# Sixteen query weights fetched and split by two GpSimd transfers each, in a two-block transformer kernel on one core

## The chip, the cores and the metric

The kernel runs on one core of a Trainium2 chip. The core has TensorE (matmuls), VectorE, ScalarE, GpSimd and SyncE, each with an instruction queue of its own that is worked off in order, and 16 DMA engines that all queues share. The metric is the device time of one execution in microseconds (us), lower is better.

## The reference

Two transformer blocks follow each other on 256 tokens of width 1024, all in float32. The part that the change touches is the first block's pair of attentions: a windowed one with grouped queries and a differential one. Cut to that part:

```python
def first_block(x, meta_tokens, pre_mix_gain, w_in, ...):
    h = concatenate([filler, meta, x], axis=1)
    u = rms_norm(h, pre_mix_gain)
    qa, ka, va, qb, kb, vb, g = split(u @ w_in, SPLITS)     # qa, qb: 1024 columns each
    qa, ka, qb, kb = (rope(t, pos) for t in (qa, ka, qb, kb))
    o_swa = windowed_gqa_sink_attention(qa, ka, va, attn_sink, pos, is_real)   # 16 heads of 64
    o_diff = differential_attention(qb, kb, vb, lam, lambda_init, ...)         # 8 pairs of heads
    gates = sigmoid(g + b_gate)
    merged = g_swa * (o_swa @ w_branch_swa) + g_diff * (o_diff @ w_branch_diff)
    h = h + rms_norm(merged @ w_out, post_mix_gain)
    ...                                                     # feed-forward, then the second block
```

The query columns qa and qb are computed in 16 pieces of 128 columns, eight each.

## The kernel before

Weights come from DRAM in tiles of 128 partitions by 1024 float32 (512 KB), which is 128 output columns for all 1024 inputs. Most products keep float32 precision with matmuls on a rounded type (float32r): a weight `raw` is split into `wh`, its rounded value, and `wl`, the rounded rest, and the activations into `uh` and `ul` in the same way. A product of 256 tokens is then 24 matmuls: for each of eight blocks `uh` times `wh` and `ul` times `wh`, and after those 16, eight of `uh` times `wl`.

- `raw_w` (L297 to L300) issues the load of a weight on SyncE's queue.
- `load_w` (L302 to L312) makes the split: ScalarE writes `wh` (L309), VectorE writes `wl` as `raw` less `wh` (L311). `raw`, `wh` and `wl` have three slots each, used in turn by all weights of the program, so the fourth weight waits until the first one's matmuls have read it.
- `gemm` (L314) calls `load_w` and issues the 24 matmuls (L325). `gemm_whole` (L333) uses `raw` unsplit, in float32 (L341); the keys' weights go that way.
- `query` (L661) makes one query piece: `gemm`, then `rope` (L505: ScalarE copies the result to `rawq`, VectorE shuffles it, GpSimd does `ropem`, `rot` and the sum), then a split into `qh` and `ql`.

The first attention has 16 units in the order `ddssdsddsdssddss` (d: a pair of heads of the differential attention, s: one of the windowed one). `prepare` (L740) makes the weights' products of a unit (for d: keys, values and query; for s: query) two units ahead of the unit that uses them; some units are followed by products for the gates. The written order is a start only: a list scheduler orders the instructions of each engine when the program is built, by its own account of what they cost, and that order is then fixed. So a change of one engine's work can move instructions on every engine.

Of the kernel before, what the change touches and what calls it, by code (L numbers as in the profile page):

```python
# [16 lines left out]
F32 = mybir.dt.float32  # L17
F32R = mybir.dt.float32r
I32 = mybir.dt.int32
BF16 = mybir.dt.bfloat16  # L20
AF = mybir.ActivationFunctionType
OP = mybir.AluOpType
# [3 lines left out]
P = 128  # L26
# [5 lines left out]
KT = D // P  # L32
# [189 lines left out]
def _program(tc, d, out):  # L222
    nc = tc.nc
    ctx = ExitStack()
    pe, act, dve, pool, sp = nc.tensor, nc.scalar, nc.vector, nc.gpsimd, nc.sync

    def new_pool(stack, name, bufs=1, space=None, side=None):
        kw = {} if space is None else {"space": space}
        if side is not None:
            kw["side"] = side  # L230
        return stack.enter_context(tc.tile_pool(name=name, bufs=bufs, **kw))

    with ctx:
        act.preload_act_table_set(EXP_LN)
        cpool = new_pool(ctx, "const")
        wpool = new_pool(ctx, "w")
# [48 lines left out]
        def split(h, l, src, gain=None):  # L285

            if gain is None:
                m = act.activation(h, src, AF.Copy)
                dve.tensor_tensor(l, src, h.bitcast(F32), OP.subtract)
            else:  # L290
                m = act.activation(h, src, AF.Copy, scale=gain)
                dve.scalar_tensor_tensor(l, src, gain, h.bitcast(F32), OP.mult, OP.subtract)  # L292
            return m

        wcount, wshare, last_w = [0], [0], [None]

        def raw_w(src, n):  # L297
            raw = wpool.tile([P, KT * P], F32, name="raw", tag="raw", bufs=3)
            last_w[0] = sp.dma_start(raw[:, :n * P], src)
            return raw  # L300

        def load_w(src, kt, c=P, raw=None, tag=""):  # L302

            if raw is None:
                raw = raw_w(src, kt)
            h = wpool.tile([P, KT * P], F32R, name="wh", tag="wh" + tag, bufs=3)
            l = wpool.tile([P, KT * P], F32R, name="wl", tag="wl" + tag, bufs=3)
            wcount[0] += 1
            act.activation(h[:, :kt * c], raw[:, :kt * c], AF.Copy)  # L309
            eng = pool if wshare[0] and wcount[0] % wshare[0] == 0 else dve  # L310
            eng.tensor_tensor(l[:, :kt * c], raw[:, :kt * c], h[:, :kt * c].bitcast(F32), OP.subtract)  # L311
            return h, l  # L312

        def gemm(src, xs, n, use, first=True, last=True, ps=None, raw=None, late=(), zero=None):  # L314


            kt = len(xs)
            h, l = load_w(src, kt, raw=raw)
            if ps is None:
                ps = mm.tile([P, 512], F32, name="mm", tag="mm")  # L320
            o = ps[:, :n]
            soon = [k for k in range(kt) if k not in late]
            steps = [(w, k, i) for ks in (soon, late) for w, i2 in ((h, 2), (l, 1)) for k in ks for i in range(i2)]
            for n_, (w, k, i) in enumerate(steps):
                pe.matmul(o, w[:, k * P:(k + 1) * P], xs[k][i], start=(first and n_ == 0),  # L325
                          stop=(last and n_ == len(steps) - 1))
                if zero is not None and n_ == 3:
                    pe.matmul(o, zero, xs[k][i][:96], start=False, stop=False)
            if last and use is not None:
                use(o)  # L330
            return ps
# [173 lines left out]
        def rope(o, dst, c, s, n, eng=pool):  # L505
            rot = kpool.tile([P, NK], F32, name="rot", tag="rot", bufs=2)
            raw = kpool.tile([P, NK], F32, name="rawq", tag="rawq", bufs=RB)
            act.activation(raw[:, :n], o, AF.Copy)  # L508
            dve.stream_shuffle(rot[:, :n], raw[:, :n], SWAP)
            m = kpool.tile([P, NK], F32, name="ropem", tag="ropem", bufs=2)  # L510
            pool.tensor_tensor(m[:, :n], raw[:, :n], c, OP.mult)  # L511
            eng.tensor_tensor(rot[:, :n], rot[:, :n], s, OP.mult)
            pool.tensor_tensor(dst, m[:, :n], rot[:, :n], OP.add)
# [3 lines left out]
        def bank():  # L517

            began[0] += 1
            return ppool.tile([P, 512], F32, name="s", tag="s") if began[0] <= 3 else None  # L520
# [140 lines left out]
        def query(src):  # L661
            q = [kpool.tile([P, NT], F32R, name="q" + e, tag="q" + e, bufs=3) for e in "hl"]

            def use(o):
                qr = kpool.tile([P, NT], F32, name="qraw", tag="qraw", bufs=2)
                rope(o, qr, cqt, sqt, NT)
                split(*q, qr)
            gemm(src, us, NT, use, ps=bank())
            return q

        oss = [None] * 8
# [53 lines left out]
        def gate_of(j):  # L725
            gemm(d["w_gate1"][j], us, NT,
                 lambda o: dve.tensor_tensor(gate[:, j, :], o, rs[:, :NT], OP.mult))
# [12 lines left out]
        def prepare(n):  # L740
            t, i = units[n]
            if t == "d":
                keys_b(i)
                values_b(i)
            qs.append(query(d["w_qb" if t == "d" else "w_qa"][i]))
            if t == "s" and i == 0:
                swa_keys()
# [15 lines left out]
                    branch_d(j)  # L763
        for j in fill:
            gate_of(j)
        wshare[0] = 0
        first = [None]

        def open_gates(j):
# [37 lines left out]
        def mem_values(groups):  # L807
            for g in groups:
                ps = [mm.tile([P, 512], F32, name="mm", tag="mm") for _ in range(2)]
                for kh in range(2):  # L810
                    h, l = load_w(d["w_xv"][g][:, kh * 1024:(kh + 1) * 1024], KT)
                    for tb in range(2):
                        tok = slice(tb * P, (tb + 1) * P)
                        for k in range(4):
                            kk_ = 4 * kh + k
                            cols = slice(k * NT, (k + 1) * NT)
                            o = ps[tb][:, :NT]
                            pe.matmul(o, mem_h[:, kk_, tok], h[:, cols], start=(kk_ == 0), stop=False)  # L818
                            pe.matmul(o, mem_l[:, kk_, tok], h[:, cols], start=False, stop=False)  # L819
                            pe.matmul(o, mem_h[:, kk_, tok], l[:, cols], start=False, stop=(kk_ == 7))  # L820
                for tb in range(2):
                    dve.tensor_scalar(vx[:, tb, g * NT:(g + 1) * NT], ps[tb][:, :NT], rsm_t[:, tb:tb + 1], None,
                                      OP.mult)
# [5 lines left out]
        for j in range(8):  # L829
            def use(o, j=j):  # L830
                t = mpool.tile([P, NT], F32, name="mt", tag="mt", bufs=2)
                dve.tensor_tensor(t, o, gate[:, j, :], OP.mult)
                dve.tensor_tensor(t, t, bd[:, j, :], OP.add)
                split(m_h[:, j, :], m_l[:, j, :], t)
# [742 lines left out]
        for h in range(4):  # L1577
# [6 lines left out]
            for qb in range(2):  # L1584
# [9 lines left out]
                l = xpool.tile([P, 1], F32, name="l1", tag="l1", bufs=4)  # L1594
# [60 lines left out]
        for k in range(FT):  # L1655
            w = load_w(d["w_dn"][k], KT, tag="" if k < FT - LAST else "_last")
            if k < FT - LAST:
                for i in range(len(parts)):
                    down(k, *w, i)
            else:  # L1660
                held.append((k, *w))
# [51 lines left out]
```

## Time and profile before

| | |
|---|---|
| median of 3 runs | 992.06 us (989.26 to 992.2) |
| the profiled execution | 991.08 us, of which 988.8 us from the first to the last instruction |
| TensorE matmul busy | 967.2 us (98%) |
| VectorE busy | 686.8 us (69%) |
| ScalarE busy | 545.3 us (55%) |
| GpSimd busy | 223.4 us (23%) |
| mean granted TensorE clock | 0.994 of full |

The first attention fills the span from about 13 us to 273 us. The profile gives, for each engine, when its instructions ran and what ended the idle time ahead of them. Matmuls overlap and their ends are modelled, so TensorE's busy share does not say that it runs at its best pace; the count of matmuls per stretch tells more.

### The profile page before, as it was taken

Reading aid. Unit: us, or ns where it says so; the run is one execution under the profiler, and the core shown is the slowest. Engines: PE = TensorE matmul, PEld = TensorE weight load, DVE = VectorE, ACT = ScalarE, POOL = GpSimd, SP = SyncE. Lnnn points to the kernel's source line nnn. Section 1 sums busy time; section 2 is a strip of 40 time slices with the busy share of each in tenths; the row PEclk is TensorE's granted clock in tenths of the full one; section 3 lists DMA queues with packets and bytes.
Section 4 is the critical chain, followed back from the end, with each engine's and each line's share of the span. In section 5 each row is a group of like instructions: output and inputs, shape, how many; then the busy total and the mean of one; then the engine's idle time right before and its main releaser. Section 6 shows DMA issues by size and latency. Waiting matters only on the chain.

```text
span 988.8 us, 18641 instructions
## 1 busy us (share of the span) xinstructions
PE 967.2 (98%) x7218; PEld 902.1 (91%) x7218; DVE 686.8 (69%) x1466; ACT 545.3 (55%) x1097; POOL 223.4 (23%) x258
## 2 busy tenths in 40 slices
PE   9999999999999999999999899999999999999996
PEld 8888998998988989999999788887799999999885
DVE  6788789888655777666554639967687686666544
ACT  5566566667554756555545344335666565555443
POOL 5534326232240123121100312121021102222002
PEclk9999999999999999999999899999999999999999
DMA  6433333332436566555675242333045255555551
GB/s 231 164 110 105 124 113 128 105 120 96 152 124 193 171 209 195 193 195 192 215 212 187 86 132 83 129 107 107 1 164 188 97 191 190 195 192 193 192 192 64
DMA packets 42023, 149.26 MB, mean 151 GB/s; under 512 B 4728, under 2 KB 5376, under 8 KB 41808
## 3 DMA queue, kind: packets, MB, share of 16 engines
q1 hardware_dynamic: 40896, 145.47, 44.4%
q0 software_dynamic: 608, 2.03, 0.7%
q8 instruction: 56, 0.92, 0.4%
q10 hardware_dynamic: 432, 0.59, 0.2%
q14 instruction: 31, 0.25, 0.1%
HBM read 147.01 MB, written 1.06 MB: 150 GB/s over the span
## 4 chain that ended last, share of the span: by engine, by line
PE 56%; DVE 8%; ACT 2%; issue 1%; DMA 0%; ACTq 0%; DVEq 0%
PE mm L325 36%; PE mm L341 4%; PE s L325 2%; PE ac L1651 2%; PE ac L1650 2%; PE ac L1647 2%; DVE fg L868 1%; DVE wl L311 1%; PE mm L1410 1%; PE mm L820 1%; PE mm L818 1%; PE mm L819 1%; DVE ul L292 1%; DVE y L1011 1%; DMA raw<-w_xq 0%
## 5 line engine op out<-in xcount | busy, mean ns | idle before, releaser
L309 ACT ACTIVATE wh<-raw 128x1024 fp32r<-128x1024 f32 (+1 forms) x232 | 243.6, 1052 | 199.7 <-PE mm L325 115.7
L311 DVE TENSOR_TENSOR wl<-raw,wh 128x1024 fp32r<-128x1024 f32 (+1 forms) x232 | 286.9, 1238 | 94.1 <-ACT wh L309 89.6
L325 PE MATMUL mm<-uh,wh 128*128 128x256 f32 (+1 forms) x1040 | 253.1, 282 | 0.0
L325 PE MATMUL mm<-ul,wh 128*128 128x256 f32 (+1 forms) x1040 | 251.2, 281 | 0.2 <-DVE ul L292 0.2
L325 PEld LDWEIGHTS mm<-uh,wh 128*128 128x128 f32 x1040 | 195.5, 188 | 2.9 <-issue 1.4
L325 PEld LDWEIGHTS mm<-ul,wh 128*128 128x128 f32 x1040 | 195.7, 188 | 0.8 <-DVE ul L292 0.4
L325 PE MATMUL mm<-uh,wl 128*128 128x256 f32 (+1 forms) x1040 | 148.6, 281 | 0.0
L325 PEld LDWEIGHTS mm<-uh,wl 128*128 128x128 f32 x1040 | 131.9, 188 | 0.5 <-issue 0.2
L341 PE MATMUL mm<-u,raw 128*128 128x256 f32 (+1 forms) x464 | 109.7, 387 | 0.0
L894 POOL TENSOR_TENSOR sg<-sg,rs 128x256 f32<-128x256 f32 x44 | 49.6, 1129 | 223.4 <-ACT sg L893 182.1
L341 PEld LDWEIGHTS mm<-u,raw 128*128 128x128 f32 x464 | 85.5, 190 | 14.3 <-issue 1.1
L898 DVE TENSOR_TENSOR ft<-mm,sg 128x256 f32<-128x256 f32 x42 | 17.8, 424 | 46.5 <-PE mm L325 44.7
L325 PE MATMUL mm<-f_h,wh 128*128 128x256 f32 x176 | 41.1, 276 | 0.0
L325 PE MATMUL mm<-f_l,wh 128*128 128x256 f32 x176 | 41.1, 276 | 0.0
L1650 PE MATMUL ac<-wh,f_l 128*128 128x512 f32 (+1 forms) x110 | 38.0, 346 | 0.0
L1651 PE MATMUL ac<-wl,f_h 128*128 128x512 f32 (+1 forms) x110 | 37.8, 347 | 0.0
L1647 PE MATMUL ac<-wh,f_h 128*128 128x512 f32 (+1 forms) x110 | 37.8, 343 | 0.0
L892 DVE TENSOR_TENSOR sg<-mm,rs 128x256 f32<-128x256 f32 x40 | 17.0, 424 | 26.1 <-PE mm L325 26.1
L325 PEld LDWEIGHTS mm<-f_h,wh 128*128 128x128 f32 x176 | 33.0, 188 | 0.0
L325 PEld LDWEIGHTS mm<-f_l,wh 128*128 128x128 f32 x176 | 33.0, 188 | 0.0
L511 POOL TENSOR_TENSOR ropem<-rawq,cqt 128x256 f32<-128x256 f32 x16 | 18.4, 1152 | 59.9 <-ACT rawq L508 59.8
L341 PE MATMUL mm<-os,raw 128*128 128x256 f32 x128 | 28.2, 380 | 0.0
(545 smaller groups left out, 2090.9 us busy)
## 6 DMA issues: line engine op xcount, KB each, us to landing
raw<-w_gu SPq DMA_DIRECT2D x88, 512.0 KB, 4.3
raw<-w_dn SPq DMA_DIRECT2D x22, 512.0 KB, 3.5
raw<-w_pr SPq DMA_DIRECT2D x20, 512.0 KB, 3.5
raw<-w_gate SPq DMA_DIRECT2D x16, 512.0 KB, 3.5
raw<-w_out SPq DMA_DIRECT2D x16, 512.0 KB, 3.7
raw<-w_fo SPq DMA_DIRECT2D x16, 512.0 KB, 3.7
raw<-w_kb SPq DMA_DIRECT2D x8, 512.0 KB, 3.5
raw<-w_vb SPq DMA_DIRECT2D x8, 512.0 KB, 3.5
```

Source lines behind the costliest of these rows:

```text
L292: dve.scalar_tensor_tensor(l, src, gain, h.bitcast(F32), OP.mult, OP.subtract)
L309: act.activation(h[:, :kt * c], raw[:, :kt * c], AF.Copy)
L311: eng.tensor_tensor(l[:, :kt * c], raw[:, :kt * c], h[:, :kt * c].bitcast(F32), OP.subtract)
L325: pe.matmul(o, w[:, k * P:(k + 1) * P], xs[k][i], start=(first and n_ == 0), stop=(last and n_ == len(steps) - 1))
L341: pe.matmul(o, raw[:, k * P:(k + 1) * P], x, start=(k == 0), stop=(k == len(xs) - 1))
L511: pool.tensor_tensor(m[:, :n], raw[:, :n], c, OP.mult)
L892: dve.tensor_tensor(sg, o, rs, OP.mult)
L894: pool.tensor_tensor(sg, sg, rs, OP.mult)
L898: dve.tensor_tensor(t, o, sg, OP.mult)
L1647: m = pe.matmul(o, f_h[:, k, tok], h[:, cols], start=(k == 0), stop=False)
L1650: pe.matmul(o, f_l[:, k, tok], h[:, cols], start=False, stop=False)
L1651: pe.matmul(o, f_h[:, k, tok], l[:, cols], start=False, stop=(k == FT - 1))
```

## The change

For the 16 query pieces alone (`query` sets a flag around its `gemm`), `load_w` no longer loads `raw` and no longer uses VectorE. GpSimd's queue issues a transfer from DRAM straight to `wh`, which is declared float32r, so the transfer converts. ScalarE then writes the negative of `wh` to `wl`, and GpSimd's queue issues a second transfer of the same 512 KB from DRAM that is added to what stands in `wl`. All other weights are loaded and split as before. The rest of the diff takes out a counter that had no effect.

```diff
-        wcount, wshare, last_w = [0], [0], [None]
+        last_w, dma = [None], [False]
...
         def load_w(src, kt, c=P, raw=None, tag=""):
 
+            h = wpool.tile([P, KT * P], F32R, name="wh", tag="wh" + tag, bufs=3)
+            l = wpool.tile([P, KT * P], F32R, name="wl", tag="wl" + tag, bufs=3)
+            h_, l_ = h[:, :kt * c], l[:, :kt * c]
+            if dma[0]:
+                pool.dma_start(h_, src)
+                act.activation(l_, h_.bitcast(F32), AF.Copy, scale=-1.0)
+                pool.dma_start(l_, src, accum_op=OP.add)
+                return h, l
             if raw is None:
                 raw = raw_w(src, kt)
-            h = wpool.tile([P, KT * P], F32R, name="wh", tag="wh" + tag, bufs=3)
-            l = wpool.tile([P, KT * P], F32R, name="wl", tag="wl" + tag, bufs=3)
-            wcount[0] += 1
-            act.activation(h[:, :kt * c], raw[:, :kt * c], AF.Copy)
-            eng = pool if wshare[0] and wcount[0] % wshare[0] == 0 else dve
-            eng.tensor_tensor(l[:, :kt * c], raw[:, :kt * c], h[:, :kt * c].bitcast(F32), OP.subtract)
+            act.activation(h_, raw[:, :kt * c], AF.Copy)
+            dve.tensor_tensor(l_, raw[:, :kt * c], h_.bitcast(F32), OP.subtract)
             return h, l
...
+            dma[0] = True
             gemm(src, us, NT, use, ps=bank())
+            dma[0] = False
```

The lines of the changed kernel stand up to six lines further down than the same lines before (the matmuls of `gemm` are L329 there, the parts of `rope` L515 to L517).

The scheduler orders the start of the first attention anew. On GpSimd, right after the eight squares `s0` of the input (L457), stood the ropes of the first keys and queries; the numbers in the names tell tiles of one name apart (`rawq_347` is the first query, `rawq_371` the second head's keys):

```order
L457 TENSOR_TENSOR s0_156<-hT_71 128x272
L511 TENSOR_TENSOR ropem_263<-rawq_260,ckt_189 128x272
L511 TENSOR_TENSOR ropem_350<-rawq_347,cqt_193 128x256
L513 TENSOR_TENSOR kraw_258<-ropem_263,rot_259 128x272
L512 TENSOR_TENSOR rot_346<-rot_346,sqt_194 128x256
L513 TENSOR_TENSOR qraw_345<-ropem_350,rot_346 128x256
```

In the changed kernel the same place on GpSimd reads (`wh_315` and `wl_316` are the first query's weight, `wh_426` and `wl_427` the second's, `wh_549` and `wl_550` the third's; `rawq_346` is the first query):

```order
L308 DMA wh_315<-w_qb 128x1024
L310 DMA wl_316<-w_qb 128x1024
L308 DMA wh_426<-w_qb 128x1024
L515 TENSOR_TENSOR ropem_263<-rawq_260,ckt_189 128x272
L517 TENSOR_TENSOR kraw_258<-ropem_263,rot_259 128x272
L308 DMA wh_549<-w_qa 128x1024
L310 DMA wl_427<-w_qb 128x1024
L515 TENSOR_TENSOR ropem_349<-rawq_346,cqt_193 128x256
L515 TENSOR_TENSOR ropem_373<-rawq_370,ckt_189 128x272
L516 TENSOR_TENSOR rot_345<-rot_345,sqt_194 128x256
L310 DMA wl_550<-w_qa 128x1024
L517 TENSOR_TENSOR kraw_368<-ropem_373,rot_369 128x272
```

The next row is the first query's `qraw`. Six issues of transfers have come in ahead of it, and each issue of a `wl` waits there for ScalarE's negative.

On ScalarE the logarithm and the exponential of the input norm's inverse root (L361, L362, `rs_a`) stood next to each other:

```order
L361 ACTIVATE rs_a_163<-st_126,base_72 128x272
L362 ACTIVATE rs_a_163<-rs_a_163 128x272
L309 ACTIVATE wh_385<-raw_383 128x1024
L309 ACTIVATE wh_429<-raw_427 128x1024
L508 ACTIVATE rawq_347<-s_314 128x256
```

In the changed kernel ScalarE's place reads:

```order
L365 ACTIVATE rs_a_163<-st_126,base_72 128x272
L309 ACTIVATE wl_316<-wh_315 128x1024
L366 ACTIVATE rs_a_163<-rs_a_163 128x272
L314 ACTIVATE wh_382<-raw_384 128x1024
L288 ACTIVATE kb_h_247<-kraw_258 128x272
```

The first query's negative, which needs the landing of `wh_315`, has come in between the two.

On TensorE the changed kernel has, where the first query's last matmuls and, further down, the third query's stand (`kb_h_247` with `qh_312` are the first scores; `wh_382` is the second head's value weight):

```order
L345 MATMUL mm_359<-u_96,raw_357 128x272 x3
L329 MATMUL mm_388<-uh_97,wh_382 128x272
L329 MATMUL mm_388<-ul_98,wh_382 128x272
L329 MATMUL s_314<-uh_97,wl_316 128x256 x7
L572 MATMUL t_302<-base_72,vT0_216 128x128
```

```order
L329 MATMUL mm_431<-uh_97,wl_427 128x256 x8
L329 MATMUL mm_554<-ul_98,wh_549 128x256
L540 MATMUL s_469<-kb_h_247,qh_312 128x272
L540 MATMUL s_470<-kb_h_247,qh_312 128x272
L540 MATMUL s_488<-kb_h_247,qh_312 128x272
L329 MATMUL mm_554<-uh_97,wl_550 128x256 x8
```

Before, `wl` of the first query followed its `wh` at once, ahead of the second head's keys; and the third query's 24 matmuls stood together. In the changed kernel keys and value matmuls, and scores, have moved in between. From the first gates' branch on, TensorE's order is that of before.

## Rows read from the trace of the kernel before

**Rows 1.** The page's first part: busy time of each engine over the whole span.
```profile
PE 967.2 (98%) x7218; PEld 902.1 (91%) x7218; DVE 686.8 (69%) x1466; ACT 545.3 (55%) x1097; POOL 223.4 (23%) x258
```

**Rows 2.** Windows: two of the first attention, one of the feed-forward.
```profile
core 0: us, PE busy (x) PEld busy (x) DVE busy (x) ACT busy (x) POOL busy (x), PEclk, DMA share, GB/s
25.00:50.00 25.00, 25.00 (x166) 21.46 (x164) 20.00 (x46) 14.03 (x36) 13.71 (x15) 1.00 0.46 159
225.00:250.00 25.00, 25.00 (x192) 22.57 (x191) 21.14 (x53) 17.33 (x46) 7.81 (x11) 1.00 0.28 94
400.00:425.00 25.00, 25.00 (x223) 25.00 (x222) 15.69 (x23) 13.67 (x19) 4.89 (x5) 1.00 0.58 191
```

**Rows 3.** Groups by line, TensorE, 13 to 246 us: the only one with idle time.
```profile
L616 PE MATMUL o<-pl,vb_h 128*128 128x256 f32 x16 | 4.6, 287 | 0.5 <-DVE pl L607 0.5
```

**Rows 4.** Groups by line, whole span: the two halves of the split.
```profile
L311 DVE TENSOR_TENSOR wl<-raw,wh 128x1024 fp32r<-128x1024 f32 (+1 forms) x232 | 286.9, 1238 | 94.1 <-ACT wh L309 89.6 <-ACT sq L646 1.9 <-ACT qx_h L288 1.3
L309 ACT ACTIVATE wh<-raw 128x1024 fp32r<-128x1024 f32 (+1 forms) x232 | 243.6, 1052 | 199.7 <-PE mm L325 115.7 <-PE ac L1650 24.2 <-issue 12.1
```

**Rows 5.** DMA issues: queue, count, size, median us from issue to landing.
```profile
raw<-w_qb SPq DMA_DIRECT2D x8, 512.0 KB, 3.5
bt<-scr POOLq DMA_DIRECT2D x1, 1024.0 KB, 7.4
base<-const_b POOLq DMA_DIRECT2D x1, 384.0 KB, 6.3
scr<-rtab POOLq DMA_DIRECT2D x1, 12.0 KB, 3.4
```

**Rows 6.** Timeline of GpSimd, start of the first attention (start, us, instruction, idle before).
```profile
5.28 5.66 POOL L457 TENSOR_TENSOR s<-hT 128x272 f32<-128x272 f32 x8 [1.41 <-DMA hT<-hT]
18.33 0.85 POOL L511 TENSOR_TENSOR ropem<-rawq,ckt 128x272 f32<-128x272 f32 x1 [7.39 <-DVE ckt L476]
22.05 1.50 POOL L511 TENSOR_TENSOR ropem<-rawq,cqt 128x256 f32<-128x256 f32 x1 [2.86 <-ACT rawq L508]
24.23 0.74 POOL L512 TENSOR_TENSOR rot<-rot,sqt 128x256 f32<-128x256 f32 x1
```

**Rows 7.** Timeline of ScalarE and of VectorE, same stretch.
```profile
14.03 0.49 ACT L361 ACTIVATE rs_a<-st,base 128x272 f32<-128x272 f32 x1 [0.34 <-PE st L458]
14.55 0.43 ACT L362 ACTIVATE rs_a<-rs_a 128x272 f32<-128x272 f32 x1
...
15.92 0.43 DVE L363 TENSOR_TENSOR rs_b<-rs_a 128x272 f32<-128x272 f32 x1
...
17.27 0.44 DVE L366 TENSOR_TENSOR rs<-rs_b,rs_a 128x272 f32<-128x272 f32 x1
```

**Rows 8.** Timeline of TensorE, same stretch.
```profile
13.63 0.49 PE L325 MATMUL s<-uh,wh 128*128 128x272 f32 x1
...
18.72 1.10 PE L325 MATMUL s<-uh,wl 128*128 128x256 f32 x8
19.66 3.83 PE L341 MATMUL mm<-u,raw 128*128 128x272 f32 x16
...
33.22 1.10 PE L325 MATMUL mm<-uh,wl 128*128 128x256 f32 x8
```

**Rows 9.** The tile wh, 13 to 273 us: the split's rests, first and last start.
```profile
L311 DVE TENSOR_TENSOR wl<-raw,wh x50: 1206/1226/1780, 12.1 to 269.4; 128x1024 fp32r<-128x1024 f32 x50
```

**Rows 10.** Windows around three gaps of TensorE (columns as in rows 2).
```profile
548.00:552.00 4.00, 2.62 (x22) 2.41 (x21) 4.00 (x7) 3.28 (x8) 4.00 (x5) 1.00 0.11 42
552.00:556.00 4.00, 1.50 (x7) 1.50 (x8) 3.90 (x5) 2.67 (x8) 3.90 (x4) 0.61 0.16 25
556.00:560.00 4.00, 4.00 (x22) 4.00 (x21) 2.70 (x7) 1.06 (x3) 0.00 (x0) 0.53 0.27 107
350.00:354.00 4.00, 2.64 (x18) 2.05 (x17) 4.00 (x10) 1.67 (x3) 1.96 (x4) 1.00 0.90 308
```

**Rows 11.** Waits, 13 to 246 us: engine waited for, us, times, longest.
```profile
POOL ropem L511 <- ACT rawq L508: 86.1, 19, 9.5
ACT wh L309 <- DMA raw<-w_gate: 2.8, 2, 2.3
```

More of the change, by code (lines that the diff above doesn't have):

```diff
@@ L765, in _program @@
             gate_of(j)
-        wshare[0] = 0
         first = [None]
```

## The prediction, made before the changed kernel ran

> **What bounds the kernel now.** I began with the page's busy times: TensorE 98%, VectorE 69%, GpSimd 23% [rows 1]. As a busy TensorE may still be a slow one, I then read windows. In the first attention TensorE is busy for all of both 25 us stretches shown, at 166 and 192 matmuls, against 223 in the feed-forward [rows 2]; part of that is that there are other matmuls among them (the keys' float32 ones take 3.83 us for eight [rows 8]). What counts is whether TensorE waits for the engines that the change relieves. By groups of lines, from 13 to 246 us, one TensorE group alone shows idle time, 0.5 us, released by VectorE's `pl` [rows 3]. So VectorE, 20 to 21 us busy of 25 there [rows 2], is used hard but almost never waited for. The reader should see that work taken from VectorE has next to nothing to give, while a weight that comes late stops TensorE, whose order is fixed.
>
> **What is removed.** Sixteen VectorE subtractions of 1.24 us [rows 4], 19.8 us, and 16 SyncE loads. These lie beside TensorE's work; what they give is the idle time that VectorE ended, 0.5 us [rows 3]. I take 0.5 us, with nothing as lower bound. ScalarE keeps 16 instructions of the same size (1.05 us [rows 4]), now a negation; their cost is unchanged but not their place, below.
>
> **What is added.** Thirty-two transfers of 512 KB on GpSimd's queue, and a chain. Before, from `raw` landed a weight was ready in 1.05 + 1.24 = 2.3 us, and `raw` was loaded ahead, into slots of its own. Now the chain starts when the `wh` slot is free: transfer, negation, second transfer.
>
> No row shows such a transfer. From below: SyncE's 512 KB land 3.5 us after the issue. From above: GpSimd's 1024 KB took 7.4 us. Between them lie GpSimd's 384 KB at 6.3 and its mere 12 KB at 3.4 us [rows 5]. The 6.3 us were in a stretch where the DMA engines were 90% busy [rows 10]; the attention has 28% to 46% [rows 2]. I take the middle of the two ends, 5.5 us, for the first transfer. The second also has to read what it adds to; its ends are the same, and I take 6.0 us, an estimate, as the bytes it touches lie nearer to the 1024 KB row. The Trainium skill, page "DMA: Bandwidth & Descriptors", section "Anatomy of one DMA — SWDGE (gpsimd) path", fits a GpSimd transfer as 2.0 us plus its bytes at 436 GB/s. That would be 3.2 us for 512 KB, and by it the opening below would lose under 1 us. The trace doesn't bear the fit out at the one size where it can be seen alone: 12 KB took 3.4 us [rows 5], where the fit has 2.0.
>
> **The opening.** The first three queries come so early that nothing could be loaded ahead. I walk the new order with the old durations.
> - GpSimd's squares end at 5.28 + 5.66 = 10.9 us [rows 6]. Then `wh_315` is issued: landed at 16.4.
> - ScalarE has the negation between the logarithm (14.03) and the exponential (14.55) [rows 7]. It runs from 16.4 to 17.5, so the exponential ends at 17.9 instead of 15.0. The four VectorE steps to `rs` took 15.92 to 17.71, 1.8 us [rows 7]: `rs` is there at 19.7, 2.0 us later. Values' transposes and the ropes wait for it.
> - `wl_316` is issued at 17.5: landed at 23.5. TensorE starts at 13.63; five keys' matmuls of 0.48 us come first now, then the 40 that took 13.63 to 18.72 [rows 8], three keys' and two values': 22.8 us. It waits 0.7 us.
> - From 23.5 TensorE has about 9.1 us of work: three times eight matmuls at 0.94 to 1.0 us (18.72 to 19.66 [rows 8]), 46 more at 0.12, and transposes. It reaches the first scores at 32.5.
> - These need the first query. Its product is complete at 24.5. With ScalarE's copy behind the value copies the rope starts at about 27 us: two `ropem` of 1.50 and one `rot` of 0.74 us [rows 6], to 30.7. The next row on GpSimd is the issue of `wl_550`, landed at 30.7 + 6.0 = 36.7. Behind that issue stand `kraw` and `qraw`; the issue and these two (about 0.75 each) end at 33.0, `qh` follows at 33.4. TensorE waits 0.9 us, does three scores in 0.4, and waits 2.9 us for `wl_550`. At 37.6 the third query is done.
>
> Before, it was done at 34.2 (33.22 + eight matmuls [rows 8]), with six more scores (0.8 us) behind it: 33.4 is what compares. The opening loses 4.2 us. With both transfers at 3.5 us the same walk ends 0.9 us late, with both at 7.4 us 8.9 us late. GpSimd's own time for 32 issues costs TensorE nothing elsewhere, as GpSimd sits in waits for `rawq` alone for 86.1 us of this attention [rows 11].
>
> **The rest of the attention.** Fifty split weights start from 12.1 to 269.4 us [rows 9], one per 5.25 us, so a slot comes round in 15.75 us. The slot of `wh` is free 16 matmuls into a weight's use, and `wl` is needed 16 matmuls into the next use: 15.75 us lie between. The chain is 5.5 + 1.05 + 6.0 and some 0.3 for handovers, 12.9 us. So 2.9 us are spare in the mean, and the 13 later queries are mostly hidden. Not all: the gates make the spacing uneven, and an issue waits behind ropes (19 waits for `rawq`, the longest 9.5 us [rows 11]). ScalarE already waited up to 2.3 us for a load without TensorE showing it [rows 11], so waits of that length don't count fully. I take 1 us in all; bounds: nothing, and 13 times 1 us with 7.4 us transfers, whose chain of 16.2 us is 0.4 us too long in the mean.
>
> **The clock.** After 1.4 and 2.5 us of idle TensorE in two neighbouring windows the granted clock was 0.61 and 0.53, near the lower level of 1.2 GHz, for two windows of 4 us: 0.39 x 4 + 0.47 x 4 = 3.4 us of full speed lost. After 1.4 us in one window it stayed at 1.00, 2.4 GHz [rows 10]. The opening's waits of 0.9 and 2.9 us lie close together, like the first pair. I take 2 us of the 3.4.
>
> **Sum.** 4.2 + 1 + 2 - 0.5 = 6.7 us. The profiled execution took 991.08 us in all: 997.8. That execution is 1 us under the median of 992.06, so I say **998 us**, 0.6% more. By the bounds: 0.9 + 0 + 0 - 0.5 to 8.9 + 13 + 3.4, so 991.5 to 1016.
>
> **The rivals.**
> - *Hidden.* Transfers of about 3.5 to 4.5 us. For it: SyncE's 3.5 us; the mean spare time. Against it: 3.4 us for 12 KB. The opening loses 0.9 to 2 us, nothing else: 991.5 to 993.5. It needs both transfers under about 4.7 us. The Trainium skill's fit above belongs here: by its 3.2 us the time would be about 991.5.
> - *Late all along.* The adding transfer takes 7.4 us or more, or issues stand behind GpSimd's waits. For it: 6.3 us for 384 KB, and `rawq` waits of 86.1/19 = 4.5 us each in the mean. Against it: 2.9 us spare. Opening 8.9, later queries 13, clock 4, so 991 + 26 = 1017. It decides from a chain of about 15.8 us on.
> - *Faster.* VectorE's `pl`, the rest of the probabilities, stands behind weights' splits in VectorE's queue, and TensorE's `o<-pl` waited 0.5 us for it once [rows 3]. With 19.8 us less on VectorE, each of the 16 units could give TensorE some 0.3 us that matmul counts hide (192 against 223 [rows 2]): 4.8 us, less 0.9 for the opening, 987. It decides where transfers take at most about 3.5 us and at least 0.25 us per unit come back. Against it: all other TensorE groups show no idle time at all.
>
> **How the numbers follow.** About 0.3%, 3 us, can be told from no change. Late opening 0.48, hidden 0.21, late all along 0.17, faster 0.14. The first alone spans 994 to 1004, and 0.03 of it lies within 3 us. So slower 0.45 + 0.17 = 0.62, same 0.24, faster 0.14. The range from 988.5 to 1011 leaves out about half of the faster case and half of the late one.
>
> **What would show it.** GpSimd's issues of `wh` and `wl` landing in about 5.5 and 6 us; TensorE waiting at about 23 us for `wl`, and near 33 us for `qh` and again for `wl`; `rs_a`'s exponential 3 us later; a granted clock under 1 soon after; few waits after 60 us; the end of the attention later by the loss, and the rest of the span unchanged. Landings under 4.7 us, or a first-attention end no later than 273 us, would make it wrong; so would TensorE waiting for `wl` at most of the 13 later queries.

## The result, and the profile of the changed kernel

The changed kernel took 998.81 us in the median of five runs (994.48 to 1000.73), against 991.81 us before on the same chip: ratio 1.0065, 95% interval 1.0046 to 1.0085. It is slower by 0.65%. The profiled execution took 994.48 us, the fastest of the five, with a span of 992.7 us at a mean granted clock of 0.995; the other four show 0.987 to 0.992.

First the page's busy times, and the row of its queue table for GpSimd's queue, which answer to [rows 1]:

```profile
PE 964.9 (97%) x7218; PEld 899.3 (91%) x7218; DVE 671.8 (68%) x1450; ACT 540.4 (54%) x1097; POOL 244.7 (25%) x290
q0 software_dynamic: 5216, 18.81, 8.3%
```

VectorE has 15 us less, GpSimd 21 us more, and TensorE's work is the same. Next windows of the first attention, of the kernel before and then of the changed one (columns as in [rows 2]):

```profile
13.00:34.00 21.00, 21.00 (x155) 19.51 (x154) 16.23 (x41) 9.74 (x23) 9.08 (x9) 1.00 0.51 179
34.00:60.00 26.00, 25.46 (x152) 21.16 (x152) 21.55 (x48) 15.52 (x42) 10.44 (x14) 1.00 0.45 151
60.00:246.00 186.00, 186.00 (x1389) 168.27 (x1389) 156.08 (x367) 120.90 (x311) 69.13 (x84) 1.00 0.34 111
```

```profile
13.00:34.00 21.00, 18.42 (x130) 16.99 (x129) 12.41 (x31) 9.59 (x19) 9.18 (x12) 1.00 0.87 227
34.00:60.00 26.00, 25.22 (x167) 21.64 (x166) 18.07 (x46) 12.93 (x36) 13.75 (x16) 1.00 0.61 176
60.00:246.00 186.00, 185.02 (x1375) 166.85 (x1373) 143.99 (x357) 121.39 (x316) 85.04 (x108) 1.00 0.53 145
```

TensorE's busy time falls by 2.58 us in the first 21 us, by 0.24 in the next 26 and by 0.98 in the 186 behind them: 3.8 us in all, most of it in the opening. The groups of TensorE from 13 to 246 us name the releasers of the larger waits (before, [rows 3] was the only one):

```profile
L329 PE MATMUL mm<-uh,wl 128*128 128x256 f32 (+1 forms) x312 | 47.5, 288 | 3.6 <-DMA wl<-w_qb 1.9 <-DMA wl<-w_qa 1.8
L572 PE MATMUL t<-base,vT 128*128 128x128 f32 x10 | 2.8, 278 | 0.5 <-DVE vT L570 0.5
```

So TensorE waited for the adding transfers, 3.6 us in three places. Two are in the opening; the third, 0.98 us at 82.9, is the sixth query. TensorE's timeline in the opening:

```profile
22.47 1.06 PE L329 MATMUL s<-uh,wl 128*128 128x256 f32 x7
...
29.62 0.33 PE L572 MATMUL t<-base,vT 128*128 128x128 f32 x1 [0.48 <-DVE vT L570]
...
33.81 1.20 PE L329 MATMUL mm<-uh,wl 128*128 128x256 f32 x8 [1.86 <-DMA wl<-w_qb]
34.85 0.28 PE L329 MATMUL mm<-ul,wh 128*128 128x256 f32 x1
35.06 0.52 PE L540 MATMUL s<-kb_h,qh 64*128 64x272 f32 x3
36.36 1.21 PE L329 MATMUL mm<-uh,wl 128*128 128x256 f32 x8 [0.78 <-DMA wl<-w_qa]
37.50 0.39 PE L540 MATMUL s<-kb_h,ql 64*128 64x272 f32 x2
```

The third query is done at 37.50, forecast 37.6. GpSimd's issues of the same stretch (the second is the first query's `wl`, the third the second query's, the last the third's):

```profile
10.83 0.71 POOL L308 DMA_DIRECT2D wh<-w_qb  x1
16.14 0.92 POOL L310 DMA_DIRECT2D wl<-w_qb  x1 [4.60 <-ACT rs_a L366]
...
26.49 0.89 POOL L310 DMA_DIRECT2D wl<-w_qb  x1 [1.20 <-ACT vb_h L578]
...
30.95 0.88 POOL L310 DMA_DIRECT2D wl<-w_qa  x1 [1.15 <-ACT wl L309]
```

And the transfers' median times from issue to landing, which answer to [rows 5]:

```profile
wh<-w_qb POOLq DMA_DIRECT2D x8, 512.0 KB, 4.9
wl<-w_qb POOLq DMA_DIRECT2D x8, 512.0 KB, 5.4
wh<-w_qa POOLq DMA_DIRECT2D x8, 512.0 KB, 4.2
wl<-w_qa POOLq DMA_DIRECT2D x8, 512.0 KB, 6.1
```

The second query's `wl`, issued at 26.49, was used at 33.81: 7.3 us. No load of SyncE's was issued in that time: of the 314 packets from 26.5 to 33.8 us 312 are of GpSimd's queue. What ran beside it were the third query's own transfers, `wh` to 29.50 and `wl` from 30.95. ScalarE and VectorE, where [rows 7] showed the root of the norm:

```profile
13.93 0.49 ACT L365 ACTIVATE rs_a<-st,base 128x272 f32<-128x272 f32 x1 [0.52 <-PE st L462]
14.76 1.06 ACT L309 ACTIVATE wl<-wh 128x1024 fp32r<-128x1024 f32 x1 [0.34 <-DMA wh<-w_qb]
15.72 0.41 ACT L366 ACTIVATE rs_a<-rs_a 128x272 f32<-128x272 f32 x1
```

```profile
19.71 1.23 DVE L315 TENSOR_TENSOR wl<-raw,wh 128x1024 fp32r<-128x1024 f32 x1 [2.62 <-ACT wh L314]
20.86 0.29 DVE L369 TENSOR_SCALAR rs_b<-rs_b 128x272 f32<-128x272 f32 x1
21.26 0.44 DVE L370 TENSOR_TENSOR rs<-rs_b,rs_a 128x272 f32<-128x272 f32 x1
```

The exponential comes 1.2 us late, but `rs` ends at 21.70, 4.0 us later than before: in VectorE's new order the split of a value weight stands ahead of the root's last two steps, and its `raw` was late.

At the end of the first attention, the first matmuls behind it, before and then in the changed kernel, start 2.9 us apart:

```profile
273.69 3.61 PE L341 MATMUL mm<-os,raw 128*128 128x256 f32 x16
```

```profile
276.61 3.61 PE L345 MATMUL mm<-os,raw 128*128 128x256 f32 x16
```

**Two parts.** Each execution has a span and a mean granted clock. Their product is about the time that the same work would take at full clock; what is left of the span is put down to the clock. The split is coarse: the clock is listed to a thousandth, which is 1 us of this span, and it counts some half clock behind TensorE's last matmul (before, the last 2.4 us of the span, at 0.50). So I take means over executions. Before has 983.4 and 6.6 us (23 executions on one chip); the changed kernel 987.3 and 9.2 (its five, the latter with a standard error of 1.3). The loss of 7 us is thus some 4 us of waits and some 3 us of clock; a profile at 0.995 shows little of the second.

### The profile page after: what moved, and what is told of

The parts are those of the page before. It is cut to its first block, busy times and chain, and to the rows that moved or that the text cites. A ratio compares the mean times of both kernels' runs of the same rounds, so it can differ in the third digit from the quotient of the medians.

```text
span 992.7 us, 18648 instructions
## 1 busy us (share of the span) xinstructions
PE 964.9 (97%) x7218; PEld 899.3 (91%) x7218; DVE 671.8 (68%) x1450; ACT 540.4 (54%) x1097; POOL 244.7 (25%) x290
## 4 chain that ended last, share of the span: by engine, by line
PE 56%; DVE 9%; ACT 2%; issue 1%; DMA 1%; DVEq 0%; ACTq 0%
PE mm L329 35%; PE mm L345 4%; PE s L329 2%; PE ac L1656 2%; PE ac L1655 2%; PE ac L1652 2%; DVE fg L873 1%; DVE wl L315 1%; PE mm L1415 1%; PE mm L825 1%; PE mm L823 1%; PE mm L824 1%; DVE ul L292 1%; DVE y L1016 1%; DMA raw<-w_xq 1%
## 5 line engine op out<-in xcount | busy, mean ns | idle before, releaser
L315 DVE TENSOR_TENSOR wl<-raw,wh 128x1024 fp32r<-128x1024 f32 (+1 forms) x216 | 267.4, 1239 | 94.7 <-ACT wh L314 93.2
L314 ACT ACTIVATE wh<-raw 128x1024 fp32r<-128x1024 f32 (+1 forms) x216 | 225.9, 1048 | 138.5 <-PE mm L329 78.2
L329 PE MATMUL mm<-uh,wh 128*128 128x256 f32 (+1 forms) x1040 | 254.2, 283 | 0.2 <-DVE vb_l L579 0.2
L329 PE MATMUL mm<-ul,wh 128*128 128x256 f32 (+1 forms) x1040 | 252.2, 281 | 0.7 <-DVE ul L292 0.7
L329 PEld LDWEIGHTS mm<-uh,wh 128*128 128x128 f32 x1040 | 195.6, 188 | 2.9 <-ACT wh L314 0.6
L329 PEld LDWEIGHTS mm<-ul,wh 128*128 128x128 f32 x1040 | 195.7, 188 | 1.6 <-DVE ul L292 0.9
L329 PE MATMUL mm<-uh,wl 128*128 128x256 f32 (+1 forms) x1040 | 146.3, 280 | 3.6 <-DMA wl<-w_qb 1.9
L329 PEld LDWEIGHTS mm<-uh,wl 128*128 128x128 f32 x1040 | 131.0, 188 | 4.7 <-DMA wl<-w_qa 2.4
L329 PE MATMUL mm<-f_h,wh 128*128 128x256 f32 x176 | 41.1, 276 | 0.0
L329 PE MATMUL mm<-f_l,wh 128*128 128x256 f32 x176 | 41.1, 276 | 0.0
L288 ACT ACTIVATE f_h<-ft 128x256 fp32r<-128x256 f32 x44 | 18.4, 420 | 37.1 <-DVE ft L903 37.1
L898 ACT ACTIVATE sg<-sg 128x256 f32<-128x256 f32 x44 | 18.2, 419 | 31.9 <-DVE sg L897 31.9
L329 PEld LDWEIGHTS mm<-f_h,wh 128*128 128x128 f32 x176 | 33.0, 188 | 0.0
L329 PEld LDWEIGHTS mm<-f_l,wh 128*128 128x128 f32 x176 | 33.0, 188 | 0.0
```

The lines of the kernel that those rows point to most:

```text
L314: act.activation(h_, raw[:, :kt * c], AF.Copy)
L315: dve.tensor_tensor(l_, raw[:, :kt * c], h_.bitcast(F32), OP.subtract)
L898: act.activation(sg, sg, AF.Silu)
```

## The experiments

All were timed in five rounds beside the kernel before on the same chip; the last two columns are the two parts just explained, means over executions (before in these runs: 983.2 to 983.9, and 5.5 to 6.6). By the standard errors a difference from before is good to about 0.5 us in the first and 1 us in the second, 2 us for the change again.

| run | us | before | ratio, 95% interval | at full clock | clock |
|---|---|---|---|---|---|
| the change again | 1003.64 | 991.77 | 1.0101 (1.0064 to 1.0139) | 988.1 | 12.7 |
| first three queries only | 998.83 | 991.77 | 1.0065 (1.0043 to 1.0087) | 988.4 | 8.6 |
| from the fourth on | 990.91 | 991.77 | 0.9985 (0.9969 to 1.0) | 982.7 | 6.2 |
| from the fourth, without the sixth | 990.42 | 991.98 | 0.9988 (0.9975 to 1.0002) | 982.9 | 5.9 |
| first query only | 993.35 | 991.98 | 1.0025 (1.0008 to 1.0043) | 984.3 | 7.5 |
| first transfer issued early | 997.46 | 991.77 | 1.0055 (1.0039 to 1.007) | 987.2 | 8.5 |
| first three, converting transfer alone | 995.81 | 991.98 | 1.0042 (1.0026 to 1.0059) | 987.6 | 6.5 |
| first three, adding transfer alone | 997.29 | 991.46 | 1.0055 (1.004 to 1.007) | 986.6 | 8.8 |
| first three, negative by VectorE | 997.15 | 992.92 | 1.0052 (1.0033 to 1.0071) | 989.4 | 6.2 |
| extra plain transfer, unused | 992.65 | 991.46 | 1.0014 (1.0004 to 1.0024) | 983.9 | 6.8 |
| extra converting transfer, unused | 992.38 | 992.92 | 0.9997 (0.998 to 1.0014) | 984.0 | 5.9 |
| `raw` loaded by GpSimd | 991.21 | 991.46 | 0.9994 (0.998 to 1.0007) | 982.6 | 6.5 |

**Where: the opening or the thirteen later queries.** The theory is my walk: the first three queries lose, the rest hides it. The rival is that all are late. Two kernels split the change, and one is the changed kernel again; each edit is one line in `query`:

```diff
-            dma[0] = True
+            nq[0] += 1
+            dma[0] = nq[0] > 3        # the other kernel: nq[0] <= 3
```

Queries four to sixteen only:

> The transfers stay for the 13 later queries; the first three queries' weights are loaded and split as before the change. If the loss lies in the opening, where nothing can be loaded ahead, this is within 3 us of the kernel before (989 to 995 us), TensorE has no wait over 1 us before 50 us, and at most one of about 1 us later on. If the loss is spread over all queries, 13/16 of it stays: 996 to 998 us. If it comes from the DMA traffic, also 13/16 of it.

The first three only:

> The transfers for the first three queries only, all others as before the change. If the loss lies in the opening, nearly all of it stays: 996 to 1000 us, with TensorE waits of about 2 us and 1 us for wl between 30 and 38 us. If it is spread over the queries or comes from the traffic, 3/16 of it stays: 992 to 994 us.

The changed kernel again:

> The changed kernel once more, with a profile of another execution. The four other executions were 4 us slower than the profiled one and had a lower mean granted clock. If the clock is the rest of the loss, a profile of a typical execution (998 to 1000 us) shows the same waits in the opening and one more stretch of granted clock 0.5 of some 3 to 7 us; if something else differs, it shows longer transfers or waits at the same clock.

The first three carry the whole loss, 1.0065 again, and the thirteen later ones none that can be told. The changed kernel beside them is at 1.0101, with an interval that overlaps; at full clock the two are alike (988.4 and 988.1), and what differs is the clock. In the kernel with the later ones TensorE has one wait from 13 to 246 us:

```profile
L329 PE MATMUL mm<-uh,wl 128*128 128x256 f32 (+1 forms) x317 | 48.7, 288 | 0.9 <-DMA wl<-w_qa 0.9
```

That is the sixth query's again, and its 0.9 us cannot be seen in the time. These thirteen also take 18 us off VectorE (668.5 busy in the profile, 686.8 before), and by the interval at most 3 us come back, perhaps nothing.

The kernel with the first three, and the changed kernel again, show what follows the waits. Windows of the first, around the clock's fall, and of the second around two falls:

```profile
35.00:38.50 3.50, 1.89 (x15) 1.62 (x15) 1.42 (x5) 0.00 (x0) 0.97 (x2) 1.00 0.71 207
38.50:42.00 3.50, 3.50 (x9) 2.65 (x9) 2.39 (x6) 1.91 (x4) 2.07 (x2) 0.51 0.08 15
```

```profile
32.00:35.40 3.40, 1.47 (x9) 0.86 (x8) 3.09 (x7) 0.74 (x2) 1.53 (x4) 1.00 1.01 207
35.40:38.80 3.40, 3.40 (x15) 2.88 (x15) 0.00 (x0) 0.11 (x1) 0.56 (x1) 0.50 0.63 237
80.00:86.60 6.60, 3.71 (x31) 3.45 (x29) 3.42 (x13) 3.19 (x11) 0.31 (x1) 1.00 0.66 153
86.60:93.40 6.80, 6.80 (x26) 5.42 (x25) 4.88 (x11) 4.89 (x14) 5.05 (x7) 0.50 0.60 128
```

Each time TensorE was idle for 1.6 to 2.9 us in a stretch and the granted clock was half in the next, for 3.4 or 6.8 us: 1.7 or 3.4 us lost. In the second kernel the sixth query's wait alone brought the 6.8 us.

**The sixth query left out as well** (`dma[0] = nq[0] > 3 and nq[0] != 6`):

> The transfers for queries 4, 5 and 7 to 16: the sixth, the only late one at which the run from the fourth on showed a TensorE wait (1.1 us), goes back to the old split. If such a wait counts in full, 1 us less than that run, so 988.5 to 991 us and 0.1% to 0.3% under the kernel before; if it is made up elsewhere, the same 990 to 992 us. If VectorE's relief is worth something of its own, it shows here as a time under the kernel before by over 0.3%.

It is the best of these versions, and not to be told from before.

**The first query alone** (`dma[0] = nq[0] == 1`):

> The first query alone by transfers. In the profile of the changed kernel the first wl landed just as TensorE came to it and the input norm's exponential ran 1.2 us later than before, so by the chain theory this costs 1 us at most: 991 to 993.5 us. If each of the three first queries costs its third of the 7 us, 994 to 995 us; if the delay of the norm by the negation ahead of it is what counts, 995 us or more.

At full clock it lies 1.1 us above before, where the walk for the first query had 0.7; but the wait is another, 1.2 us for VectorE's `vT`. `rs` is late here too (it ends at 22.35); that this is the reason is not shown.

**The first transfer issued ahead of the squares**, so that it lands before its negation is due:

```diff
+        early.append(wpool.tile([P, KT * P], F32R, name="wh", tag="wh", bufs=3))
+        tc.keep_in_program_order(pool.dma_start(early[0], d["w_qb"][0]))
...
+                if not landed_early[0]:
+                    pool.dma_start(h_, src)
```

> All 16 queries by transfers, but the first query's converting transfer is issued ahead of GpSimd's squares, at about 4 us instead of 10.8. If the chain of transfers in the opening sets the loss, the first wl is no longer late and the exponential of the input norm is not held: 2 us or more come back, 993 to 997 us, while the third query's wl still waits for GpSimd's rope. If the opening doesn't matter, it stays at 998 to 1000 us; if the traffic at the start matters, it is slower than that, as the transfer now meets the loads of the input.

At 997.46 us it lies just above the range expected. The transfer was issued at 3.82, among the loads of the input, and the waits only moved. TensorE's two groups with waits:

```profile
L332 PE MATMUL mm<-uh,wh 128*128 128x256 f32 (+1 forms) x312 | 84.5, 301 | 2.8 <-DVE vb_l L584 2.8
L332 PE MATMUL mm<-uh,wl 128*128 128x256 f32 (+1 forms) x311 | 48.0, 288 | 1.6 <-DMA wl<-w_qa 1.6
```

**One transfer instead of two.** For the first three queries `wh` comes by the converting transfer, and VectorE subtracts it from a `raw` that SyncE loads:

```diff
-                act.activation(l_, h_.bitcast(F32), AF.Copy, scale=-1.0)
-                pool.dma_start(l_, src, accum_op=OP.add)
+                raw = raw_w(src, kt)
+                dve.tensor_tensor(l_, raw[:, :kt * c], h_.bitcast(F32), OP.subtract)
```

> First three queries only: wh by GpSimd's converting transfer as in the change, but raw is loaded as before and VectorE subtracts, so the second transfer, the negation and GpSimd's wait for it are gone, while the bytes from DRAM stay doubled. If two transfers in series make the weights late, most of the 7 us of the run with the first three queries comes back: 991 to 994 us and no TensorE wait over 1 us before 50 us. If the doubled traffic in the opening is the cause, or a GpSimd transfer there as such, it stays at 996 to 1000 us.

A miss: the waits for `wl` are gone, and 3.8 us stay. TensorE's waits are elsewhere now:

```profile
L620 PE MATMUL o<-ph,vb_h 128*128 128x256 f32 x16 | 4.9, 306 | 1.5 <-ACT ph L610 1.5
L572 PE MATMUL t<-base,vT 128*128 128x128 f32 x10 | 2.8, 284 | 0.2 <-DVE vT L570 0.2
```

Three things could be behind that: the second fetch of the same bytes, GpSimd's transfer as such, or the new order. The next kernels take them one at a time, with the first three queries split as before. Ahead of that split stands one addition, or one replacement:

```diff
+                spare = wpool.tile([P, KT * P], F32, name="spare", tag="spare", bufs=2)
+                pool.dma_start(spare[:, :kt * c], src)      # unused; then as before
```

> Every weight is loaded and split as before the change; for each of the first three queries GpSimd's queue also fetches the 512 KB once more, into a tile that nothing reads. So only the traffic of a second fetch is there, and its three issues of about 0.6 us on GpSimd. If the 4 us that were left with one converting transfer per query came from traffic that holds up the other loads of the opening: 994.5 to 996.5 us, and raw loads there that land 6 us or more after their issue. If they came from the weight that GpSimd fetches being late itself: 991 to 993 us, as before. I think the second likelier, 0.6, as the mean share of the DMA engines in that stretch was 0.72 and not 1.

The same with `spare` of the rounded type, in which every engine's order is that of the run with the plain one:

> As the run with the traffic alone, in the same order on every engine, but the extra 512 KB of each of the first three queries go into a tile of the rounded type, so that the unused transfer converts. With one converting transfer in use the loss was 3.8 us, with the plain unused one 1.2 us. If converting itself loads the DMA engines or holds up the other loads: 994 to 996 us. If what was left came from the order of the engines and from wh being late: 991.5 to 993.5 us, as with the plain one. I think the second likelier, 0.75.

And `raw` of the three loaded by GpSimd instead of SyncE (`raw = wpool.tile(...)`, `pool.dma_start(raw[:, :kt * c], src)`):

> Weights are split as before the change (ScalarE writes wh, VectorE wl), with the same bytes; only the loads of raw for the first three queries are issued by GpSimd's queue, behind its squares, instead of SyncE's. If traffic makes the rest of the loss: 991 to 993 us, as before. If it is the transfer that GpSimd issues (later than SyncE's, and 4 to 6 us long): 993.5 to 996 us, with the first query's wh on ScalarE starting only at about 15 us and the exponential of the norm's root behind it.

None of the three costs more than 1.2 us (0.14%, for the plain unused transfer), and at full clock all lie within 1 us of before. So three more fetches, converting or not, and GpSimd's queue as such do not make the loss. But the scheduler moved these transfers too: the unused ones were issued at 3.8 (two) and 11.4 or 11.1 us, where the changed kernel issues at 10.8, 18.4 and 24.7, and GpSimd's first `raw` at 6.15, ahead of seven of the eight squares. From 13 to 34 us the DMA engines were busy for 0.62 and 0.64 of the time with the unused transfers, 0.72 with the converting ones in use, 0.87 in the changed kernel. Traffic at the queries' own time is thus not excluded, and no unused adding transfer was tried. That the loss needs a weight for which TensorE, or an engine ahead of it, has to wait is argued and not shown by these three.

**The adding transfer alone.** SyncE loads `raw` and ScalarE writes `wh` as before; only `wl` is made the new way:

```diff
-                pool.dma_start(h_, src)
+                raw = raw_w(src, kt)
+                act.activation(h_, raw[:, :kt * c], AF.Copy)
```

> For the first three queries SyncE loads raw and ScalarE writes wh as before the change; only wl is made by the new way: ScalarE writes the negative and GpSimd's transfer from DRAM is added. ScalarE has three instructions of 1.05 us more in the opening. If the two transfers in series make the loss, one of them alone still leaves 6 us from the negative to wl, against 1.2 us of VectorE before: a wait for the first queries' wl of 1 to 2 us and 993 to 996 us. If the late first transfer alone made it: 991.5 to 993 us. If any extra GpSimd fetch in the opening costs 4 us: 995 to 997 us, with landings of raw of 6 us or more.

The time is 5.8 us over before, above every range expected, although the negation ran at 13.69, ahead of the logarithm, and `rs` ended at 17.41, 0.3 us earlier than in the kernel before. TensorE's group with the wait:

```profile
L330 PE MATMUL mm<-uh,wl 128*128 128x256 f32 (+1 forms) x312 | 50.4, 290 | 2.2 <-DMA wl<-w_qb 2.2
```

The first two adding transfers took 8.6 us in the median, and from 10 to 40 us SyncE's four `raw<-w_kva` 5.9, against 3.7 before. So here the transfers were slow beside each other; whether the adding ones also cost time by slowing SyncE's loads, no run separates.

**The negative by VectorE** instead of ScalarE (`dve.tensor_scalar(l_, h_.bitcast(F32), -1.0, None, OP.mult)`):

> The two transfers as in the change for the first three queries alone, but VectorE writes the negative of wh instead of ScalarE, so that the logarithm and the exponential of the norm's root stand next to each other on ScalarE again and three of ScalarE's instructions of 1.05 us are gone. If the negation's place on ScalarE (the root 1.2 us late in the changed kernel, and ropes and value copies behind it) carries the loss: 993 to 995 us. If the two transfers in series carry it, the chain stays at 5 + 1.2 + 6 us: 996.5 to 999 us, as with ScalarE's negative in the first three queries (998.83 us), and TensorE still waits 1 to 2.5 us for a wl. I think the second likelier, 0.7.

The root is on time (`rs` ends at 18.29), and 4.2 us stay. The reason is read on VectorE and then on TensorE:

```profile
28.56 0.71 DVE L309 TENSOR_SCALAR wl<-wh 128x1024 fp32r<-128x1024 f32 x1 [2.10 <-DMA wh<-w_qa]
30.04 0.43 DVE L570 TENSOR_TENSOR vT<-mm,rs 128x272 f32<-128x272 f32 x1
```

```profile
30.53 0.33 PE L572 MATMUL t<-base,vT 128*128 128x128 f32 x1 [1.36 <-DVE vT L570]
```

The negation waits for the converting transfer at the head of VectorE's queue, the values' `vT` stands behind it, and TensorE waits for that. The `wl` waits have shrunk to 0.3 and 0.2 us; the chain is paid in another place. The profile's waits from 13 to 246 us, 2.3 us, are less than half of the 5.5 us lost at full clock.

## Why the prediction was right

- **The bound.** TensorE's order is fixed and it almost never waited for VectorE: shown by the kernels with the thirteen later queries and without the sixth, which run at 0.9985 (0.9969 to 1.0) and 0.9988 (0.9975 to 1.0002). The rival with 4.8 us did not appear: the second interval leaves room for 2.5. Whether the 0.5 us that I put down as gain is there cannot be told; both kernels lie 0.9 and 1.6 us under before.
- **The transfers.** 5.5 and 6.0 us were forecast; the medians were 4.9 and 4.2 for the converting one, 5.4 and 6.1 for the adding one. The 6.3 us for 384 KB that I had weighed [rows 5] says little of size: four more issues stood right behind it, and the one of 1 KB took 6.0 us. The rival of hidden transfers needed both under 4.7 us; the adding one is not, though one of the two converting medians is. The Trainium skill, page "DMA: Bandwidth & Descriptors", section "Anatomy of one DMA — SWDGE (gpsimd) path", fits 2.0 us plus the bytes at 436 GB/s, an estimate of 3.2 us for 512 KB; no median here comes under 4.2, so the trace does not agree for these transfers.
- **The opening, 4.2 us.** The total held: the third query was done at 37.50 (forecast 37.6), and the kernel with only these three queries changed is 5.0 us longer at full clock. That it held so closely is in part luck, as the places within it were partly wrong. No wait came for the first `wl` (0.7 us forecast): its `wh` landed by 14.76, 1.6 us earlier than my 16.4. Nor did the scores wait for `qh` ahead of the third `wl`. Instead the second query's `wl`, which I had not priced, took 7.3 us and cost 1.86 us, which put the scores back to 35.06. The wait for the third `wl` was then 0.78 us, not 2.9.
- **The root.** I had `rs` 2.0 us late, from the negation on ScalarE alone. It was 4.0 late, as VectorE's order had changed too and I had walked ScalarE's, GpSimd's and TensorE's only. The exponential was 1.2 us late, not the 3 that I named as a sign. It mattered little: with the root on time the loss stayed at 4.2 us, and in the kernel whose `raw` GpSimd loads `rs` ended at 21.83, without a loss.
- **The rest of the attention, 1 us.** Measured as nothing (983.4 at full clock before, 982.7 with the thirteen). The spare time of 2.9 us in the mean was enough, but for the sixth query's wait of 0.8 to 2.9 us and, with the first transfer issued early, one more of 0.8 us at 168. The first attention ended 2.9 us later, the span 3.9; nothing here explains the last 1 us.
- **The clock, 2 us.** About right with the first three queries alone (2.1 us) and in the changed kernel (2.6, standard error 1.3), too small for its second measurement (6.1). I had taken a share of one fall; after waits of this length the clock fell twice in the first attention of one profiled execution and not at all in that of the other. With the converting transfer alone and with VectorE's negative, whose longest waits were 1.5 and 1.4 us, it cost nothing (0.2 and -0.2 us). My reading of [rows 10] was loose: that fall began at 552.9, so 1.6 of the 2.5 us of idle time lay within it and not ahead of it.

The sum, 6.7 us, met the measured 7.0 in part by luck: the waits came out a little smaller (some 4 us against 4.7) and the clock a little larger. The changed kernel's two measurements, 1.0065 and 1.0101, differ mainly in the clock, and their intervals overlap.

**What stays open.** The converting transfer alone costs 4.4 us at full clock, of which its profile shows 1.7 us as waits of TensorE. Three unused transfers early in the opening and GpSimd's issue are excluded; what is left is the order of the engines around a `wh` that comes late, and the traffic at that time, and no run separates these. A version of the two transfers in the order of before was not tried.

## What to carry to other kernels

A transfer that replaces an engine's work was free here where a weight is fetched a slot ahead, and was paid where the first weights are needed at once: keep the old way for the first few, and read the gain, if any, from whether anyone waited for the relieved engine. When such a chain has an instruction in its middle, ask what stands behind that instruction in its engine's queue, on every engine whose order has moved. Give a few short waits of TensorE a range and not one price: in the kernels that lost 3.0 to 5.5 us at full clock, the clock added between nothing and 6 us.

## What the runs showed of the hardware

The adding transfer keeps the DMA engines busier than a plain one of equal size. GpSimd's queue in the page's queue table (packets, MB, share of 16 engines): before, with three plain transfers more, three converting, three adding, and three of each of the latter two:

```profile
q0 software_dynamic: 608, 2.03, 0.7%
q0 software_dynamic: 1040, 3.60, 1.1%
q0 software_dynamic: 1040, 3.60, 1.2%
q0 software_dynamic: 1040, 3.60, 1.5%
q0 software_dynamic: 1472, 5.18, 2.1%
```

A share of 0.1% of some 990 us is 1 us, so one transfer of 512 KB takes all engines for about 1.3 us plain (0.4% by three), 1.6 converting and 2.6 adding, each give or take 0.3 by the rounding. (The kernel whose three `raw` GpSimd loads, plain too, has 1.2%, so plain and converting cannot be told apart.) In the opening that shows as a share of 0.93 at 245 GB/s with the adding transfers alone, against 0.72 at 246 GB/s with the converting ones (windows of these two kernels):

```profile
13.00:34.00 21.00, 18.56 (x133) 17.33 (x132) 10.77 (x31) 10.87 (x19) 8.24 (x10) 1.00 0.93 245
```

```profile
13.00:34.00 21.00, 20.83 (x153) 19.28 (x153) 14.95 (x33) 6.42 (x16) 8.82 (x9) 1.00 0.72 246
```

In the opening an issue on GpSimd took 0.55 to 0.71 us for the converting and 0.88 to 0.92 us for the adding transfer.
